# Two blocks in one kernel: the first convolution's weights and taps, and the even mixer's token stage

## The chip, the cores and the metric

One core of a Trainium2 chip runs the whole program. The metric is the device time of one execution in microseconds, as the median of several runs. A profiled execution gives the trace from which the views below are taken; its span runs from the first to the last instruction.

## The reference, cut to what matters

One sequence of 512 tokens with 1024 channels passes through two blocks of two layers each, in float32. The change touches the first layer of either block.

```python
def conformer_conv(x, ...):               # first block, first layer
    a, b = split(rmsnorm(x, g) @ pw1_w + pw1_b, 2)
    h = a * sigmoid(b)
    h = depthwise_causal_conv(h, dw_w) + dw_b      # 31 taps per channel
    h = silu(layernorm(h, ln_g, ln_b))
    return h @ pw2_w + pw2_b

def even_mixer(h, ...):                   # second block, first layer
    z = h @ w_in                          # u, v, q, k, vv and the forget logits
    u, v = gelu(z[..., :512]), gelu(z[..., 512:1024])
    log_f = log_sigmoid(f_logit + b_f)
    q, k = rms_norm(q, g_qn), rms_norm(k, g_kn)    # per head of 64
    y_a = u * (w_s . rms_norm(v) + b_s)   # inside blocks of 128 tokens
    y_b = softmax(q.k / 8 + c_t - c_s, causal) . vv, c = cumsum(log_f)   # 8 heads
    return concat(y_a, y_b) @ w_out
```

The first block ends with `rmsnorm(h, final_norm)`, and the second begins with `rms_norm(x, g_mix)`.

## The kernel before, in words

The stream x is held transposed: eight tiles of 128 channels by 512 tokens. Every product of full precision is done as three matmuls of fp32r halves, `mm3` (lines 242 to 245): high x high, high x low and low x high. `split` (lines 260 to 262) makes the two halves of a tile, the high one with ScalarE and the low one with VectorE. `wload` (from line 215) brings a weight tile with one transfer on SP's queue and splits it; the raw tiles have three buffers, the halves two.

The order of the instructions isn't the program's. The tile framework plans each engine's queue with a simulated timeline and takes, among what is ready, what stands first in the program. `behind(last)` (line 256) puts the instructions of its block behind `last` on that engine's queue. PSUM has eight banks of 128x512, which `banks` deals out to tags.

**Convolution** (lines 600 to 732). Eight chunks of x are loaded; `Norm.chunk` (from line 332) splits each, scaled by the gain, and sums the squares, partly on GpSimd, partly on ScalarE. The two weight tiles of block 0 are loaded on the same queue after chunks 1 and 4. `front(c)` does the two products of output block c (48 matmuls into two banks of tag "acc", which has three), multiplies both by R, the row of 1/rms per token, and gates them into `hp`. Block 0 comes without R: `rest()` loads the taps, forms the token sums with 128x1 matmuls (`token_sums`, line 279) and spreads the factors into R. `back(c)` does the 31 taps of block c. PE_TAPS of them run on TensorE, as three matmuls with a diagonal matrix that ScalarE makes from the identity (lines 655 and 656); then VectorE adds its taps into the same PSUM bank (tag "o", two banks; line 665), while GpSimd adds POOL_TAPS of products that ScalarE makes (lines 667 to 673). Line 677 joins both sums into `yc[c]` and so frees the bank. For the last block VectorE sums into `z`, so that it need not wait for TensorE, and line 675 joins it to GpSimd's `y`. Between the blocks TensorE also multiplies the memory's keys and values (tag "m", two banks), for later layers. Then follow the layer norm and the second product.

**Even mixer** (lines 1009 to 1205). `n4` is the norm between the blocks, with an outer factor: the first block's final norm has to be applied to x itself, and r0 is its 1/rms. `factors` forms both sums and r, r0; `row` spreads r into R and r0 into R0, and GpSimd multiplies the eight x by R0 (line 370). `token_linear` (line 1036) multiplies tokens by weights into four banks of tag "tok" (five); its weights come in four quarters of 24 matmuls. The first one is v. `head_norm` (from line 1054) takes such a product, scales it by r, sums squares by head on GpSimd and VectorE, and normalises. In order of the program: v, u, keys, queries, forget gates, the gating by `w_s`, values. `rsqrt` uses a power on GpSimd and four small VectorE operations (lines 273 to 277).

The attention's logits of a head (`weights`, line 736) are, for each of four query tiles, three matmuls into a bank of tag "s": two for q.k, from xh and xl, and one for the cumulated forget gate, with `selh` as the selecting matrix and `cs` as the values. `cs` has rows 0 to 7 and 32 to 39, in a tile of 64 partitions; the rest of it is zero. The query tiles have 128, 256, 384 and 512 columns. Then VectorE adds the mask and takes the minimum, ScalarE the exponential, GpSimd scales, TensorE transposes and applies the values (`apply`, line 759). The products with the first half of `w_out` have no need of the heads and fill TensorE between them.

Of the kernel before, what the change touches and what calls it, by code (L numbers as in the profile page):

```python
# [15 lines left out]
S = 512  # L16
D = 1024
DC = 8
# [4 lines left out]
PE_TAPS = (10,) * 5 + (12, 14, 18)  # L23
POOL_TAPS = (6,) * 8
# [109 lines left out]
def tile_kernel(ctx, tc, I, out):  # L134
# [9 lines left out]
    def nm(s):  # L144
        uid[0] += 1
        return f"{s}_{uid[0]}"
# [25 lines left out]
    def tmp(shape, tag, bufs=None, dt=FT, pool=None):  # L172
        return (pool or tp).tile(shape, dt, tag=tag, name=nm(tag), bufs=bufs)
# [105 lines left out]
    def token_sums(accs, n=S // 128, o=None):  # L279

        o = ps(n, tag="st") if o is None else o
        for j in range(n):
            for i, acc in enumerate(accs):
                T.matmul(o[:, j:j + 1], acc[:, j * 128:(j + 1) * 128], ones[:, 0:1], start=i == 0, stop=i == len(accs) - 1)
        return o
# [35 lines left out]
    class Norm:  # L321
# [17 lines left out]
        def factors(self, last=None):  # L339
# [18 lines left out]
            if self.outer:  # L358
                V.tensor_tensor(self.r, self.r, self.r0, op=OP.mult)

        def row(self, R=None, parts=False, last=None):

            with behind(last):
                R = tmp([128, S], "R", 1) if R is None else R
                A.activation(R, spread(self.r, parts=parts), AF.Copy)
                if self.outer:
                    R0 = tmp([128, S], "t", TB)
                    A.activation(R0, spread(self.r0), AF.Copy)
                    for c in range(DC):
                        G.tensor_tensor(x[c], x[c], R0, op=OP.mult)  # L370
            return R

# [228 lines left out]
    first = []  # L601
    for c in range(DC):
        nc.sync.dma_start(x[c], I["xt"][c])
        if c in (1, 4):
            first.append(wload(I["w_pw1"][0, len(first)], 8, 128))
        n0.chunk(c)
    n1 = Norm("ffn_norm", 0, quick=())
    with phase("conv") as p, banks(acc=3, st=1, o=2, m=2):
        yc = [p.tile([128, S], FT, name=f"yc{c}") for c in range(DC)]
        s1, s2, mark = [], [], {}  # L610
        with phase("conv_a") as q:
# [6 lines left out]
            def rest():  # L618
                nc.sync.dma_start(wd, I["taps"])
                split(wdh, wdl, wd)  # L620
                n0.finish(R)

            def front(c):

                o = []
                for j in range(2):
                    w = wload(I["w_pw1"][c, j], 8, 128) if c else first[j]
                    o.append(ps())
                    lin(o[j], w, xh, xl)
                if c == 0:  # L630
                    rest()
                sb = tmp([128, S], "t", TB)
# [376 lines left out]
    with phase("even") as p, banks(t=2):  # L1009

        selh = p.tile([64, 8, 128], FR, name="selh")
# [7 lines left out]
        cs = p.tile([64, S], FR, name="cs")  # L1019
# [5 lines left out]
        with banks(tok=5, st=1):  # L1025
            with phase("even_p") as q:
# [9 lines left out]
                def token_linear(src):  # L1036

                    o = [ps(tag="tok") for _ in range(4)]
                    for u in range(4):
                        wh, wl = wload(src[u], 2, 512)  # L1040
                        for k in range(2):
                            for j in range(4):
                                t = slice(128 * j, 128 * j + 128)
                                last = mm3(o[j], xh[:, 2 * u + k, t], xl[:, 2 * u + k, t], wh[:, k], wl[:, k], u + k == 0, u == 3 and k == 1)
                        token_linear.last.append(last)
                    return o

                token_linear.last = []
                first = token_linear(I["w_em"][0])
                n4.factors(token_linear.last[0])  # L1050
                R = n4.row(parts=True, last=token_linear.last[3])
# [60 lines left out]
                head_norm(token_linear(I["w_em"][1]), 8, AF.Copy, queries)  # L1112
                with phase("even_f") as q2:
# [299 lines left out]
```

## Time and profile before

| | before |
|---|---|
| runs, us | 2489.91, 2494.72, 2497.57 (median 2494.72) |
| profiled execution, us | 2492.68 |
| its span, us | 2490.8 |
| TensorE busy | 2435.1 us, 98% |
| weight loads busy | 2112.4 us, 85% |
| VectorE busy | 2027.5 us, 81% |
| ScalarE busy | 1272.5 us, 51% |
| GpSimd busy | 396.7 us, 16% |
| granted TensorE clock, mean | 0.993 |

The profiled execution's own time is 1.9 us more than its span. Busy shares are means over the whole kernel; the views below are taken from the stretches that change, in us from the span's start. PE is TensorE, PEld its weight loads, DVE VectorE, ACT ScalarE, POOL GpSimd, SP the engine that issues transfers. The matmuls overlap: a row's duration is longer than the step to the next one, so their pace is read from the starts.

### The profile page before, as it was taken

To read this page: it belongs to the slowest core of one execution; us is meant where nothing else is said; L and a number is where in the kernel's file an instruction comes from. 1 tells how busy PE (TensorE), PEld (TensorE's weight loads), DVE (VectorE), ACT (ScalarE), POOL (GpSimd) and SP (SyncE) were. 2 spreads that over 40 slices of the span, in tenths; PEclk is the share of its full clock that TensorE was granted. 3 is DMA by queue.
4 is the path that set the end of the run, shared out by engine and by line. 5 is a ranking of instruction groups with operands and counts; after the bars stand their busy time and mean duration, and the time that the engine had idled before them with its cause. 6 is when DMAs were issued, how large, how long until landed. Compare 5 with 4: busy or idle time off the path is not lost.

```text
span 2490.8 us, 37986 instructions
## 1 busy us (share of the span) xinstructions
PE 2435.1 (98%) x14133; PEld 2112.4 (85%) x14133; DVE 2027.5 (81%) x3511; ACT 1272.5 (51%) x2182; POOL 396.7 (16%) x444
## 2 busy tenths in 40 slices
PE   8998999999999999999999999999999999999999
PEld 6876899998777879999977778899999888799998
DVE  6896899886688869998765877799987766899885
ACT  6674544444577845444453566644444325644442
POOL 3781000000134400000014544000000014000000
PEclk9999999999999999999999999999999999999999
DMA  4122333332400033333322123333333222333332
GB/s 139 60 68 85 106 100 113 103 102 73 130 30 15 1 98 94 111 106 105 100 77 76 51 68 132 124 105 105 103 102 106 69 92 94 97 101 108 102 102 77
DMA packets 82712, 226.11 MB, mean 91 GB/s; under 512 B 9440, under 2 KB 20192, under 8 KB 82272
## 3 DMA queue, kind: packets, MB, share of 16 engines
q1 hardware_dynamic: 82528, 223.69, 28.6%
q8 instruction: 112, 1.84, 0.3%
q14 instruction: 72, 0.59, 0.1%
HBM read 216.31 MB, written 4.19 MB: 89 GB/s over the span
## 4 chain that ended last, share of the span: by engine, by line
PE 86%; DVE 7%; POOL 2%; issue 2%; ACT 1%; DMA 1%; SPq 0%; DVEq 0%; POOLq 0%; ACTq 0%
PE fi L244 12%; PE fi L245 12%; PE fi L243 12%; PE fo L243 6%; PE fo L244 6%; PE fo L245 6%; PE acc L245 6%; PE acc L243 6%; PE acc L244 6%; PE s L746 2%; DVE wl L262 2%; PE tok L244 1%; PE tok L245 1%; PE t L769 1%; PE tok L243 1%
## 5 line engine op out<-in xcount | busy, mean ns | idle before, releaser
L261 ACT ACTIVATE wh<-wr 128x1024 fp32r<-128x1024 f32 (+2 forms) x435 | 360.4, 833 | 595.8 <-PE fo L244 184.7
L262 DVE TENSOR_TENSOR wl<-wr,wh 128x1024 fp32r<-128x1024 f32 (+2 forms) x431 | 419.3, 975 | 95.6 <-ACT wh L261 91.5
L244 PE MATMUL fo<-hl,wh 128*128 128x512 f32 x704 | 275.2, 391 | 0.0
L245 PE MATMUL fo<-hh,wl 128*128 128x512 f32 x704 | 275.0, 391 | 0.0
L243 PE MATMUL fo<-hh,wh 128*128 128x512 f32 x704 | 272.8, 391 | 0.0
L243 PE MATMUL fi<-th,wsh 128*128 128x256 f32 x912 | 257.6, 282 | 0.0
L244 PE MATMUL fi<-tl,wsh 128*128 128x256 f32 x912 | 257.4, 282 | 0.0
L245 PE MATMUL fi<-th,wsl 128*128 128x256 f32 x912 | 257.2, 282 | 0.0
L245 PE MATMUL fi<-xh,wl 128*128 128x256 f32 (+1 forms) x800 | 246.9, 309 | 0.0
L244 PE MATMUL fi<-xl,wh 128*128 128x256 f32 (+1 forms) x800 | 246.7, 309 | 0.0
L262 DVE TENSOR_TENSOR wsl<-ws,wsh 128x1024 fp32r<-128x1024 f32 x152 | 185.6, 1221 | 74.9 <-ACT wsh L261 74.8
L243 PE MATMUL fi<-xh,wh 128*128 128x256 f32 (+1 forms) x800 | 245.9, 308 | 0.0
L261 ACT ACTIVATE wsh<-ws 128x1024 fp32r<-128x1024 f32 x152 | 161.1, 1060 | 73.8 <-PE fi L244 73.6
L243 PE MATMUL acc<-xh,wh 128*128 128x512 f32 x416 | 166.6, 403 | 11.6 <-ACT wh L261 9.3
L244 PEld LDWEIGHTS fi<-tl,wsh 128*128 128x128 f32 x912 | 174.1, 191 | 1.1
L245 PEld LDWEIGHTS fi<-th,wsl 128*128 128x128 f32 x912 | 174.2, 191 | 0.6
L243 PEld LDWEIGHTS fi<-th,wsh 128*128 128x128 f32 x912 | 174.1, 191 | 0.7
L501 DVE TENSOR_TENSOR x<-fo,x 128x512 f32<-128x512 f32 x192 | 131.1, 684 | 49.2 <-PE fo L245 48.4
L245 PE MATMUL acc<-xh,wl 128*128 128x512 f32 x416 | 167.5, 403 | 2.3 <-DVE wl L262 2.2
L244 PE MATMUL acc<-xl,wh 128*128 128x512 f32 x416 | 166.1, 400 | 0.0
L243 PEld LDWEIGHTS fi<-xh,wh 128*128 128x128 f32 x800 | 151.0, 189 | 12.1
L244 PEld LDWEIGHTS fi<-xl,wh 128*128 128x128 f32 x800 | 150.3, 188 | 12.2
(507 smaller groups left out, 6326.2 us busy)
## 6 DMA issues: line engine op xcount, KB each, us to landing
wr<-in_w_fin_dram SPq DMA_DIRECT2D x88, 512.0 KB, 3.5
wr<-in_w_sin_dram SPq DMA_DIRECT2D x88, 512.0 KB, 3.6
wr<-in_w_fout_dram SPq DMA_DIRECT2D x64, 256.0 KB, 2.7
wr<-in_w_sout_dram SPq DMA_DIRECT2D x64, 256.0 KB, 2.7
wr<-in_w_pw_dram SPq DMA_DIRECT2D x24, 512.0 KB, 3.7
wr<-in_w_xkv_dram SPq DMA_DIRECT2D x16, 512.0 KB, 3.6
wr<-in_w_em_dram SPq DMA_DIRECT2D x16, 512.0 KB, 3.5
wr<-in_w_fout_dram SPq DMA_DIRECT2D x32, 192.0 KB, 2.6
```

What stands on the lines that cost most here:

```text
L243: T.matmul(o, lh, rh, start=start, stop=False)
L244: T.matmul(o, lh, rl, start=False, stop=False)
L245: return T.matmul(o, ll, rh, start=False, stop=stop)
L261: A.activation(h, src, AF.Copy)
L262: V.tensor_tensor(l, src, f32(h), op=OP.subtract)
L501: V.tensor_tensor(x[m], o, x[m], op=OP.add)
L746: T.matmul(o, qs(i), keys[:, :n], start=a == 0, stop=a == len(pairs) - 1)
L769: T.transpose(ot[:, a:a + 128], tiles[i][:, 128 * j:128 * j + 128], ident)
```

## The change

In the convolution PE_TAPS goes from 94 to 104 taps in all (blocks 0 to 4 get two more each), POOL_TAPS from 48 to 46 (two fewer in the last block), and VectorE's share from 106 to 98. The two weight tiles of block 0 come in halves of four k, issued by ScalarE, ahead of the chunks in the program; their splits are of 512 columns. Block 0's two products are walked together over k. Block 1's products use the two banks "m" and stand behind block 0's token sums on TensorE.

In the even mixer the token sums of `n4` stand between the third and the last quarter of the first product, the Gelu table is loaded as soon as r is there, and `row` no longer multiplies x. That is done by `stream`, called after the queries: VectorE multiplies x by R0 in PSUM. `selh` and `cs` get 128 partitions, the new ones zero.

```diff
--- before.py
+++ after.py
@@ -20,8 +20,8 @@
 FC = 22
 EPS = 1e-6
 TAPS = 31
-PE_TAPS = (10,) * 5 + (12, 14, 18)
-POOL_TAPS = (6,) * 8
+PE_TAPS = (12,) * 6 + (14, 18)
+POOL_TAPS = (6,) * 7 + (4,)
 BIG = 1e30
 
 BLOCKS = (3, 3, 4, 4, 4, 4)
@@ -281,7 +281,8 @@
         o = ps(n, tag="st") if o is None else o
         for j in range(n):
             for i, acc in enumerate(accs):
-                T.matmul(o[:, j:j + 1], acc[:, j * 128:(j + 1) * 128], ones[:, 0:1], start=i == 0, stop=i == len(accs) - 1)
+                token_sums.last = T.matmul(o[:, j:j + 1], acc[:, j * 128:(j + 1) * 128], ones[:, 0:1], start=i == 0,
+                                           stop=i == len(accs) - 1)
         return o
 
     def spread(r, tag="st", parts=False):
@@ -357,18 +358,20 @@
             rsqrt(self.r, a, 4)
             if self.outer:
                 V.tensor_tensor(self.r, self.r, self.r0, op=OP.mult)
+            return token_sums.last
 
         def row(self, R=None, parts=False, last=None):
 
             with behind(last):
                 R = tmp([128, S], "R", 1) if R is None else R
                 A.activation(R, spread(self.r, parts=parts), AF.Copy)
-                if self.outer:
-                    R0 = tmp([128, S], "t", TB)
-                    A.activation(R0, spread(self.r0), AF.Copy)
-                    for c in range(DC):
-                        G.tensor_tensor(x[c], x[c], R0, op=OP.mult)
             return R
+
+        def stream(self):
+
+            R0 = spread(self.r0)
+            for c in range(DC):
+                V.tensor_tensor(x[c], x[c], R0, op=OP.mult)
 
         def finish(self, R=None, row=True, parts=False):
             self.factors()
@@ -598,11 +601,18 @@
 
 
     n0 = Norm("a_norm", 0, quick=(1, 3, 5))
-    first = []
+
+    first = [[wp.tile([128, 1024], dt, tag="w" + e, name=nm("w" + e), bufs=b) for e, dt, b in
+              (("r", FT, WR), ("h", FR, WH), ("l", FR, WH))] for _ in range(2)]
+    halves = slice(0, 512), slice(512, 1024)
+    for h, half in enumerate(halves):
+        for j, (raw, _, _) in enumerate(first):
+            nc.scalar.dma_start(raw[:, half].rearrange("p (k m) -> p k m", k=4), I["w_pw1"][0, j, :, 4 * h:4 * h + 4])
     for c in range(DC):
         nc.sync.dma_start(x[c], I["xt"][c])
-        if c in (1, 4):
-            first.append(wload(I["w_pw1"][0, len(first)], 8, 128))
+        if c in (0, 3):
+            for raw, hi, lo in first:
+                split(hi[:, halves[c // 3]], lo[:, halves[c // 3]], raw[:, halves[c // 3]])
         n0.chunk(c)
     n1 = Norm("ffn_norm", 0, quick=())
     with phase("conv") as p, banks(acc=3, st=1, o=2, m=2):
@@ -618,17 +628,25 @@
             def rest():
                 nc.sync.dma_start(wd, I["taps"])
                 split(wdh, wdl, wd)
-                n0.finish(R)
+                n0.factors()
+                rest.sums = token_sums.last
+                n0.row(R)
 
             def front(c):
 
-                o = []
-                for j in range(2):
-                    w = wload(I["w_pw1"][c, j], 8, 128) if c else first[j]
-                    o.append(ps())
-                    lin(o[j], w, xh, xl)
+
+                o = [ps(tag="m" if c == 1 else "acc") for _ in range(2)]
                 if c == 0:
+                    for k in range(DC):
+                        for j, (_, hi, lo) in enumerate(first):
+                            s_ = slice(128 * k, 128 * k + 128)
+                            mm3(o[j], hi[:, s_], lo[:, s_], xh[:, k], xl[:, k], k == 0, k == DC - 1)
                     rest()
+                else:
+                    for j in range(2):
+                        w = wload(I["w_pw1"][c, j], 8, 128)
+                        with behind(rest.sums if c == 1 and j == 0 else None):
+                            lin(o[j], w, xh, xl)
                 sb = tmp([128, S], "t", TB)
                 V.tensor_tensor(sb, o[1], R, op=OP.mult)
                 A.activation(sb, sb, AF.Sigmoid, bias=col("a_pw1_b", 8 + c))
@@ -1008,7 +1026,8 @@
 
     with phase("even") as p, banks(t=2):
 
-        selh = p.tile([64, 8, 128], FR, name="selh")
+        selh = p.tile([128, 8, 128], FR, name="selh")
+        G.memset(f32(selh[64:128]), 0.0)
         for a in (0, 32):
             A.activation(selh[a:a + 32], ident[a:a + 32, a:a + 8].unsqueeze(2).to_broadcast([32, 8, 128]), AF.Copy)
         mask = p.tile([128, S], FT, name="mask")
@@ -1016,7 +1035,7 @@
         G.affine_select(mask, mask, [[-1, S]], OP.is_ge, BIG, base=384, channel_multiplier=1)
         gqn = p.tile([128, 1], FT, name="gqn")
         V.tensor_scalar(gqn, col("e_g_qn_2"), -0.125, None, op0=OP.mult)
-        cs = p.tile([64, S], FR, name="cs")
+        cs = p.tile([128, S], FR, name="cs")
         G.memset(f32(cs), 0.0)
         yh = p.tile([128, 4, S], FR, name="yh")
         yl = p.tile([128, 4, S], FR, name="yl")
@@ -1033,22 +1052,24 @@
                 wsl = q.tile([128, 4, 128], FR, name="wsl")
                 split(wsh, wsl, wsr)
 
-                def token_linear(src):
+                def token_linear(src, between=None):
 
                     o = [ps(tag="tok") for _ in range(4)]
+                    last = None
                     for u in range(4):
                         wh, wl = wload(src[u], 2, 512)
-                        for k in range(2):
-                            for j in range(4):
-                                t = slice(128 * j, 128 * j + 128)
-                                last = mm3(o[j], xh[:, 2 * u + k, t], xl[:, 2 * u + k, t], wh[:, k], wl[:, k], u + k == 0, u == 3 and k == 1)
-                        token_linear.last.append(last)
+                        with behind(between(last) if between and u == 3 else None):
+                            for k in range(2):
+                                for j in range(4):
+                                    t = slice(128 * j, 128 * j + 128)
+                                    last = mm3(o[j], xh[:, 2 * u + k, t], xl[:, 2 * u + k, t], wh[:, k], wl[:, k],
+                                               u + k == 0, u == 3 and k == 1)
+                    token_linear.last = last
                     return o
 
-                token_linear.last = []
-                first = token_linear(I["w_em"][0])
-                n4.factors(token_linear.last[0])
-                R = n4.row(parts=True, last=token_linear.last[3])
+                first = token_linear(I["w_em"][0], n4.factors)
+                table(AF.Gelu_apprx_tanh, n4.r)
+                R = n4.row(parts=True, last=token_linear.last)
                 r = n4.r
 
                 def head_norm(o, groups, func, done):
@@ -1110,6 +1131,7 @@
 
                 head_norm(token_linear(I["w_em"][2]), 8, AF.Copy, keys)
                 head_norm(token_linear(I["w_em"][1]), 8, AF.Copy, queries)
+                n4.stream()
                 with phase("even_f") as q2:
                     fw = q2.tile([128, DC, 128], FR, name="fw")
                     fraw = q2.tile([128, DC, 8], FT, name="fraw")
```

## Rows read from the trace of the kernel before

**Rows 1.** Waits of TensorE, 0 to 225 us: total us, times, longest us.
```profile
PE acc L243 <- ACT wh L261: 8.5, 1, 8.5
PE o L243 <- DVE yc L677: 4.7, 1, 4.7
...
PE acc L243 <- DVE t L633: 1.9, 1, 1.9
```

**Rows 2.** Busy time by stretch, convolution: PE, PEld, DVE, ACT, POOL, clock, DMA.
```profile
40.00:160.00 120.00, 120.00 (x516) 96.56 (x516) 107.18 (x139) 85.19 (x192) 87.24 (x71) 1.00 0.22 67
160.00:180.00 20.00, 15.11 (x57) 11.60 (x56) 19.96 (x25) 15.97 (x45) 13.26 (x9) 0.83 0.14 51
```

**Rows 3.** Waits of TensorE, 1260 to 1500 us.
```profile
PE tok L244 <- DVE wl L262: 6.3, 2, 3.6
PE tok L243 <- ACT tt L1062: 3.0, 1, 3.0
```

**Rows 4.** Busy time by stretch, the two attentions (columns as in rows 2).
```profile
1410.00:1460.00 50.00, 50.00 (x244) 35.83 (x243) 34.34 (x101) 32.40 (x91) 14.87 (x30) 1.00 0.04 11
750.00:850.00 100.00, 96.79 (x582) 80.85 (x580) 85.38 (x278) 83.61 (x231) 46.96 (x86) 1.00 0.02 7
```

**Rows 5.** Timeline, convolution's last block: start, duration, engine, line, tiles, wait.
```profile
172.63 0.77 PE L243 MATMUL o<-ch,dgt 128*128 128x512 f32 x1 [4.68 <-DVE yc L677]
...
176.97 0.39 PE L244 MATMUL o<-cl,dgt 128*128 128x512 f32 x1
...
187.91 1.76 DVE L675 TENSOR_TENSOR y<-y,z 128x512 f32<-128x512 f32 x1 [3.89 <-POOL y L673]
...
189.77 0.69 DVE L677 TENSOR_TENSOR yc<-o,y 128x512 f32<-128x512 f32 x1
```

**Rows 6.** Timeline, start of the kernel.
```profile
2.17 0.43 SPq L224 DMA_DIRECT2D wr<-in_w_pw_dram  x1
...
16.82 1.41 DVE L266 SCALAR_TENSOR_TENSOR xl<-x,vec,xh 128x512 fp32r<-128x512 f32 x2
...
22.55 0.40 PE L245 MATMUL acc<-xh,wl 128*128 128x512 f32 x1
```

**Rows 7.** Groups by line, 40 to 190 us: busy us, mean ns, idle us.
```profile
L665 DVE SCALAR_TENSOR_TENSOR o<-hp,wd,o 128x512 f32<-128x512 f32 x99 | 72.2, 750 | 4.3 <-PE o L245 3.0
L673 POOL TENSOR_TENSOR y<-y,u 128x512 f32<-128x512 f32 x38 | 56.5, 1491 | 5.1 <-ACT u L672 3.9
```

**Rows 8.** Timeline, token sums and the factor r.
```profile
1284.36 1.84 PE L284 MATMUL st<-ones,acc 128*128 128x1 f32 x16
...
1291.44 0.16 DVE L359 TENSOR_TENSOR n_r<-n_r,n_r 128x4 f32<-128x4 f32 x1
```

**Rows 9.** Timeline, before and beside the multiplication of x.
```profile
1306.20 0.16 DVE L274 TENSOR_TENSOR rs_t<-rs_y 128x8 f32<-128x8 f32 x1
...
1310.89 12.02 POOL L370 TENSOR_TENSOR x<-x,t 128x512 f32<-128x512 f32 x8 [1.25 <-ACT t L368]
...
1311.07 1.25 DVE L274 TENSOR_TENSOR rs_t<-rs_y 128x8 f32<-128x8 f32 x1
```

**Rows 10.** Busy time by stretch, token stage (columns as in rows 2).
```profile
1330.00:1368.00 38.00, 38.00 (x173) 30.84 (x172) 15.65 (x25) 14.64 (x19) 11.54 (x8) 1.00 0.27 84
1368.00:1407.00 39.00, 35.37 (x179) 29.34 (x178) 37.23 (x51) 23.36 (x35) 25.96 (x16) 0.96 0.28 76
```

**Rows 11.** Tile selh (count, ns min/median/max, first to last), then the timeline beside it.
```profile
L746 PE MATMUL s<-cs,selh x32: 323/410/498, 1407.3 to 1458.0; 64*128 64x128 f32 x8, 64*128 64x256 f32 x8, 64*128 64x384 f32 x8, 64*128 64x512 f32 x8
...
1422.06 0.40 PE L746 MATMUL s<-xl,YS 128*128 128x512 f32 x1
1422.39 0.49 PE L746 MATMUL s<-cs,selh 64*128 64x512 f32 x1
1422.81 0.50 PE L775 MATMUL o<-th,V4f 128*128 128x512 f32 x1
1423.15 0.22 PE L746 MATMUL s<-xh,YS 128*128 128x128 f32 x1
```

## The prediction

> **What bounds the kernel now.** I read the waits of TensorE first, then busy time by stretch, then groups, then the timeline at each wait. In the convolution TensorE has three stops worth a name: 8.5 us before its first matmul, 1.9 us for VectorE's `t` (line 633) and 4.7 us for VectorE's `yc` (line 677) [rows 1]. Between 40 and 160 us it never stops: 516 matmuls in 120 us, 0.2326 us each, with VectorE busy for 107 us and GpSimd for 87 [rows 2]. In 160 to 180 us VectorE is full (19.96 of 20) and TensorE is not, and its granted clock is 0.83 [rows 2]. So this stage changes its bound: first TensorE's stream, then VectorE's taps. In the even mixer's token stage TensorE waits 6.3 us in two stops for the low half of a weight tile and 3.0 us for `tt` [rows 3]. In its attention no wait of note is listed, TensorE is busy 50 of 50 [rows 4], so the time there is the matmuls' own pace. A stop costs more than itself: after the 4.7 us, ten matmuls took 176.97 - 172.63 = 4.34 us instead of 2.33, at half the clock (1.2 instead of 2.4 GHz), 2.0 us more [rows 5]. After the shorter stops I take 1.5.
>
> **Convolution.** *First weights.* Today a block's split is one 1024-wide piece and block 0 runs to its end before block 1. With halves and both blocks walked together over k, TensorE can start on half a block, and its last six matmuls follow the last `xl`. That one ends at 18.23 us, so 18.23 + 6 x 0.2326 = 19.6 us is the floor for a phase that now ends at 22.95 [rows 6]: at best -3.3 us. The other end is 0, if the chunks are late anyway; nothing makes it a loss but two issues more, 0.43 us each [rows 6]. They go to ScalarE's queue, which has no transfers so far; they leave SP's, so that x's later chunks are issued two places sooner. I take -2.5, near the floor, since VectorE's chain and not the weights sets the end. The page "DMA: Bandwidth & Descriptors" of the Trainium skill (Issuing engines are not separate DMA queues) says that a second queue saves only issue time; no row here separates the two queues, and by it this term would be about 0 and the whole 2472.5.
> *Block 1 before R.* Front(1) now takes the two "m" banks, so it needs no bank that R frees: the stop of 1.9 and its slow start of 1.5 go, -3.4. If another wait took its place it would be the next bank, which R frees some 11 us (48 x 0.2326) later than the sums; R is there by then.
> *Ten taps to TensorE.* Three matmuls each, 30 x 0.2326 = +7.0 us, on an engine without a gap in 40 to 160 us: all on the path. ScalarE builds 20 more diagonals; it idles 34.8 of these 120 us [rows 2], and even at a VectorE tap's 0.75 us [rows 2, 7] they are 15, so I charge nothing; uncovered, that is up to 15.
> *VectorE's relief.* Blocks 0 to 4 lose two taps each there, 10 x 0.75 = 7.5 us [rows 7]. VectorE releases the bank for block 7's taps, and TensorE waited 4.7 for it; the two new changes ahead of it cancel the added taps for TensorE (-5.9 + 7.0), so it arrives 1.1 later and VectorE 7.5 earlier: stop and slow start go, -6.7. Ends: 0 and -6.7.
> *Tail.* Block 7 loses two GpSimd taps (2 x 1.49) and gains two VectorE ones (2 x 0.75) [rows 7]. VectorE idled 3.89 us there for GpSimd's `y`, so `yc` came at 190.46 [rows 5], while the last tap was out at about 176.97 + 44 x 0.2326 = 187.2. With `y` ready first, `yc` follows the last tap by its own 0.7 us and loses 2.2 to 2.6; I take -2.2, the other end is 0.
> Sum of the stage: -2.5 - 3.4 + 7.0 - 6.7 - 2.2 = -7.8.
>
> **Token stage.** *Sums earlier.* The token sums ran at 1284.36, after the whole first product; r was there at 1291.60 [rows 8]. They now stand before its last quarter, 24 matmuls or 5.6 us earlier, and the Gelu table is loaded once r is there instead of ahead of the first `tt`. The stop of 3.0 for `tt` goes, and 1.5 behind it: -4.5. What is queued behind the sums is that last quarter; it would wait if VectorE's sums were late. Ends 0 and -4.5; I take all of it, as 5.6 exceeds 3.0.
> *Stream factor.* GpSimd's eight multiplications took 12.02 us. Beside them a 128x8 VectorE operation took 1.25 instead of 0.16 us [rows 9], and the stop of 6.3 - 3.6 = 2.7 us for `wl` follows that jam. With them gone, -2.7 - 1.5 = -4.2. VectorE instead does 8 x 0.69 = 5.5 us (one of its 128x512 operations, the 0.69 of [rows 5]) and four scalings by the identity. In 1330 to 1368 us VectorE is busy for 15.65 of 38 us [rows 10], so I cost them at nothing: the planner has 22 us of room after r0 and before the first x is added. Without that cover they fall into 1368 to 1407, where VectorE is busy 37.23 of 39, and cost 5.5 + 1.5.
> *Third stop.* The 3.6 us [rows 3] lies in that full stretch. I leave it as it is: 0, between -5.1 (gone) and +7.0.
> Sum: -8.7. The memsets are GpSimd's, which is idle for 26 of the 38 us [rows 10]; uncovered they are one small operation each.
>
> **Attention.** A full 512-wide matmul steps 0.2326 us. The one before `selh` stepped 1422.39 - 1422.06 = 0.33, `selh` itself (64 rows) 0.42, the one behind it 0.34 [rows 11]: 0.10 + 0.19 + 0.10 = 0.39 too much, in each of 32 groups (all widths taken alike), 12.4 us. At 128 rows nothing sets these three apart from their neighbours. Upper end -12.4. The other end comes from the first block's attention, the same pipeline with no such matmul: there TensorE is busy 96.8 of 100 with VectorE and ScalarE at 85 and 84, while here they are at 69 and 65 [rows 4]. 34.34 / 0.854 = 40.2 us is what these 50 could shrink to before VectorE is as full as there, so -9.8 in 50 is near a cap; waits between heads of 1 us each would leave -4. I take -8, between the cap and that.
> The page "TensorEngine Tiling (Array Packing)" of the Trainium skill (Overview, Theoretical Speedup) speaks against this edit: a contraction of up to 64 rows can run up to twice as fast, so widening would give that up. Here the 64-row matmul took 0.42 where a full one steps 0.23, so the trace doesn't agree; the same page (Tiling Modes, Key Properties) says that a change of tiling mode drains the engine, and that the trace does show, on both sides of it.
>
> **Sum.** -7.8 - 8.7 - 8 = -24.5 us. The profiled execution took 2492.68; the median of the three runs is 2.0 above it. 2494.7 - 24.5 = 2470.
>
> **Rivals.** *Taps on the full engine* (0.13): the front is bound by x's chunks and the relief of VectorE ends in another wait (GpSimd is busy 87 of 120 us), so the stage gains nothing: 2478. For it: TensorE has no gap for 7 us. Against: VectorE is what it waited for. *Attention gives it back* (0.10): heads wait for VectorE and ScalarE as in the first block, or 64 rows are the cheaper form (half a step for 32 matmuls, some -2.5 us lost): gain 0 to 3, 2477 to 2480. *Stream in the full stretch* (0.08): +7.0, 2477. *Order elsewhere* (0.07): the planner orders the whole program anew; `behind` orders only TensorE's own queue, so the changed parts may not start when they say. Two of the gains fail or are paid back by some five new stops of 3 + 1.5: 2488 to 2494. *Slower* (0.04): with 20% of its work gone, TensorE runs dry in attention and each head becomes a chain that nothing fills, with the stop and the half clock of [rows 5], 6.7 us a head. Eight heads are +54 and the 8 lost, 2532; 2478 + 4 x 6.7 = 2505 is past the bound of 2502, so it is slower from four heads on. Against: the first block's attention keeps a granted clock of 1.00 [rows 4].
>
> **Numbers.** The forecast has 0.58, with a range of its own from 2462 to 2479 (attention between -12 and -4, the third stop, the start). The four rivals beside it end below 2481 in 0.31. A measurement of this kernel can tell 0.3%, 7.5 us, so faster means below 2487.2: 0.87, counting a little off for the tails; same 0.09, slower 0.04. The range 2461 to 2485 takes in the forecast and the first three rivals.
>
> **What would show it.** First matmul before 8.0 us; no stop near 31; no wait of `o` for `yc` line 677 above 1 us; the first matmul of the pointwise product after the convolution some 8 us before 210. In the even mixer no wait for `tt`, no GpSimd run of eight x, steps of 0.23 around `selh`, and attention some 8 us shorter. It is wrong if TensorE stops for `wl` longer than 6.3 us in the token stage, if a new wait stands at block 7, or if attention keeps its length with waits for `a_mn` or `p`.

## The result and the profile after

The changed kernel takes 2476.69 us (median of 4 runs, 2476.0 to 2477.16) against 2493.23 for the one before (4 runs): ratio 0.9932, interval 0.9915 to 0.995, so 16.5 us or 0.7% faster. The forecast was 24.5 us. The profiled execution has a span of 2474.6 us; before it was 2490.8, which leaves 16.1. Where they come from is read off the first matmul of each stage in the two timelines:

| first matmul of, us | before | after | gained so far |
|---|---|---|---|
| the first ffn (`fi`): end of the convolution | 263.73 | 264.44 | -0.7 |
| the token stage (`tok`) | 1248.15 | 1247.95 | 0.2 |
| the attention's first `selh` | 1407.29 | 1397.82 | 9.5 |
| the last values (`V4f`) of the attention | 1472.40 | 1457.07 | 15.3 |
| the next ffn | 1589.40 | 1573.73 | 15.7 |

So the convolution gave nothing, the token stage 9.3 and the attention 5.9 us; these are single profiles, and the section on the experiments says how far such times scatter. The waits of TensorE from 0 to 225 us after the change (total us, times, longest):

```profile
PE acc L243 <- ACT xh L265: 6.3, 1, 6.3
PE st L296 <- DVE t L295: 3.4, 2, 2.6
PE m L244 <- DVE wl L262: 2.7, 2, 2.4
PE st L284 <- DVE s L704: 2.6, 1, 2.6
PE m L243 <- ACT wh L261: 1.7, 1, 1.7
```

Against [rows 1] the stops for `yc` and for `t` in front of block 1 are gone, and the first matmul is 2.2 us earlier. But there are new stops: 1.7 us for `wh`, the split of block 1's weight, 2.6 for the sum `s` behind the last block, and 2.6 for `t` in front of the layer norm's second spread (line 296). The kernel before had one stop of 3.7 us at that norm, for another `t` (line 575). Busy time by stretch, the first row the first blocks, the others to be held against [rows 2, 4] (PE, PEld, DVE, ACT, POOL, clock, DMA share, GB/s):

```profile
6.00:42.00 36.00, 32.52 (x114) 23.55 (x115) 26.09 (x45) 28.89 (x61) 10.73 (x10) 0.91 0.47 164
160.00:180.00 20.00, 20.00 (x87) 16.15 (x86) 19.86 (x21) 16.46 (x48) 12.44 (x9) 1.00 0.11 35
1410.00:1460.00 50.00, 47.53 (x263) 38.80 (x262) 38.13 (x103) 36.14 (x94) 15.60 (x32) 0.97 0.13 43
```

From 160 to 180 us TensorE is now full, 87 matmuls in place of 57, at a clock of 1.00. In the attention it does 263 in 50 us in place of 244, with VectorE and ScalarE busier by some 4 us each. From 6 to 42 us it did 114 matmuls; the kernel before has this row:

```profile
6.00:42.00 36.00, 30.90 (x115) 22.99 (x116) 25.33 (x42) 25.29 (x53) 9.88 (x8) 0.95 0.49 178
```

With 115 there, the early start was spent before 42 us. The timeline of the changed kernel shows where (TensorE, then ScalarE):

```profile
21.28 0.40 PE L245 MATMUL acc<-xh,wl 128*128 128x512 f32 x1
21.51 0.95 PE L284 MATMUL st<-ones,acc 128*128 128x1 f32 x8
24.12 0.50 PE L243 MATMUL m<-xh,wh 128*128 128x512 f32 x1 [1.67 <-ACT wh L261]
24.46 0.39 PE L244 MATMUL m<-xl,wh 128*128 128x512 f32 x1
25.61 2.05 PE L296 MATMUL st<-t,ones 128*128 128x512 f32 x2 [0.76 <-DVE t L295]
26.67 1.42 PE L243 MATMUL m<-xh,wh 128*128 128x512 f32 x1
27.88 0.63 PE L244 MATMUL m<-xl,wh 128*128 128x512 f32 x1
28.31 0.63 PE L245 MATMUL m<-xh,wl 128*128 128x512 f32 x1
...
16.00 3.62 ACT L673 ACTIVATE dgt<-ident,wdh 128x128 fp32r<-128x128 f32 x12
19.52 3.61 ACT L674 ACTIVATE dgt<-ident,wdl 128x128 fp32r<-128x128 f32 x12
23.03 1.99 ACT L261 ACTIVATE wh<-wr 128x1024 fp32r<-128x1024 f32 x2
```

Block 0 ends at 21.28 instead of 22.55 [rows 6]. ScalarE, however, has 24 diagonals for block 0's twelve taps ahead of the split and gets to it only at 23.03. Then R's spread stands third in TensorE's queue and holds block 1 up; the matmuls behind it step 28.31 - 27.88 = 0.43 us instead of 0.23, at half the clock; from 6 to 42 us the granted clock is 0.91 on average.

By 180 us the changed kernel has started 706 matmuls and the one before 676: the difference is just the 30 added ones, so the two are level ahead of the last block.

At the other end of the convolution (VectorE, then GpSimd):

```profile
166.83 7.83 DVE L683 SCALAR_TENSOR_TENSOR z<-hp,wd,z 128x512 f32<-128x512 f32 x5
174.58 0.74 DVE L683 SCALAR_TENSOR_TENSOR o<-hp,wd,o 128x512 f32<-128x512 f32 x1
175.24 1.12 DVE L683 SCALAR_TENSOR_TENSOR z<-hp,wd,z 128x512 f32<-128x512 f32 x1
...
178.64 0.74 DVE L683 SCALAR_TENSOR_TENSOR z<-hp,wd,z 128x512 f32<-128x512 f32 x1
...
186.09 1.29 DVE L695 TENSOR_TENSOR yc<-o,y 128x512 f32<-128x512 f32 x2
...
172.48 5.04 POOL L691 TENSOR_TENSOR y<-y,u 128x512 f32<-128x512 f32 x3
186.86 1.26 POOL L704 TENSOR_TENSOR s<-s,yc 128x512 f32<-128x512 f32 x1 [9.35 <-DVE yc L695]
```

Block 7's own taps (`z`) stand ahead of block 6's (`o`) on VectorE. Both `yc` come at 186 to 187 us: block 7's earlier than the 189.77 of [rows 5], block 6's later than before (183.3), and it is block 6's for which GpSimd idles 9.35 us.

In the even mixer one wait of [rows 3] is left, the third stop, and `tt` is gone (waits of TensorE, 1260 to 1500 us); the tile `selh` and the steps around it answer to [rows 11]:

```profile
PE tok L244 <- DVE wl L262: 3.7, 1, 3.7
PE acc L243 <- ACT wh L261: 1.1, 1, 1.1
```

```profile
L764 PE MATMUL s<-cs,selh x32: 273/308/393, 1397.8 to 1439.8; 128*128 128x128 f32 x8, 128*128 128x256 f32 x8, 128*128 128x384 f32 x8, 128*128 128x512 f32 x8
...
1410.16 0.40 PE L764 MATMUL s<-xl,YS 128*128 128x512 f32 x1
1410.40 0.39 PE L764 MATMUL s<-cs,selh 128*128 128x512 f32 x1
1410.62 0.40 PE L793 MATMUL o<-th,V4f 128*128 128x512 f32 x1
1410.86 0.22 PE L764 MATMUL s<-xh,YS 128*128 128x128 f32 x1
```

Steps of 0.24, 0.22 and 0.24 us stand where 0.33, 0.42 and 0.34 stood.

### The profile page after: what moved, and what is told of

It is laid out like the page before. It is cut to its first block, busy times and chain, and to the rows that moved or that the text cites. A ratio compares the mean times of both kernels' runs of the same rounds, so it can differ in the third digit from the quotient of the medians.

```text
span 2474.6 us, 38058 instructions
## 1 busy us (share of the span) xinstructions
PE 2428.0 (98%) x14163; PEld 2114.0 (85%) x14163; DVE 2025.8 (82%) x3513; ACT 1276.2 (52%) x2202; POOL 375.9 (15%) x435
## 3 DMA queue, kind: packets, MB, share of 16 engines
q8 instruction: 112, 1.84, 0.3%
## 4 chain that ended last, share of the span: by engine, by line
PE 87%; DVE 6%; issue 2%; ACT 2%; POOL 2%; DMA 1%; SPq 0%; DVEq 0%; ACTq 0%; POOLq 0%
PE fi L244 12%; PE fi L245 12%; PE fi L243 12%; PE fo L243 7%; PE fo L244 7%; PE fo L245 7%; PE acc L245 6%; PE acc L243 6%; PE acc L244 6%; PE tok L244 2%; PE tok L245 2%; PE tok L243 2%; PE s L764 1%; PE t L787 1%; DVE wl L262 1%
## 5 line engine op out<-in xcount | busy, mean ns | idle before, releaser
L262 DVE TENSOR_TENSOR wl<-wr,wh 128x1024 fp32r<-128x1024 f32 (+2 forms) x433 | 425.5, 985 | 89.5 <-ACT wh L261 88.7
L243 PE MATMUL acc<-xh,wh 128*128 128x512 f32 x400 | 158.1, 400 | 7.0 <-ACT xh L265 6.3
L245 PE MATMUL acc<-xh,wl 128*128 128x512 f32 x400 | 159.7, 400 | 2.4 <-DVE wl L262 2.4
L244 PE MATMUL acc<-xl,wh 128*128 128x512 f32 x400 | 159.6, 399 | 0.8 <-DVE xl L266 0.8
```

Of the source, the lines that this page charges most:

```text
L243: T.matmul(o, lh, rh, start=start, stop=False)
L244: T.matmul(o, lh, rl, start=False, stop=False)
L245: return T.matmul(o, ll, rh, start=False, stop=stop)
L262: V.tensor_tensor(l, src, f32(h), op=OP.subtract)
```

## The experiments

Every kernel was timed in five rounds beside the kernel before, and ratios are to that. The times of the reordered versions lie within 6 us of each other and their intervals overlap, so what tells them apart is the stage in the trace. There the first ffn starts between 263.30 and 265.58 us in the five profiles with the changed kernel's convolution, and between 263.36 and 266.12 in the three with the one before.

**The two halves of the change.** The first has only the convolution's hunks of the diff above, the second only the even mixer's, the third only this:

```diff
-        selh = p.tile([64, 8, 128], FR, name="selh")
+        selh = p.tile([128, 8, 128], FR, name="selh")
+        G.memset(f32(selh[64:128]), 0.0)
...
-        cs = p.tile([64, S], FR, name="cs")
+        cs = p.tile([128, S], FR, name="cs")
```

> The kernel before with the convolution part of the change alone (first weights by halves, both blocks together, block 1 in the m banks, the new tap tables). Theory: in the changed kernel the first matmul of the first ffn starts 0.7 us later than before, so the convolution part as a whole gains nothing: the span stays within 2 us of before, ratio 0.9995 to 1.001, and the same two new stops show, one near 23 us for the split of block 1's weights and one near 187 us for the sum with the last yc. Rival: the parts are planned together and spoil each other; alone the convolution gains the 7.8 us that were forecast, ratio 0.997.

> The kernel before with the even mixer's part alone (sums before the last quarter, x scaled by VectorE after the queries, the selecting matrix and its values on 128 partitions). Theory: it carries the whole gain, 9 to 10 us in the token stage and 6 in the attention, so the span is 15 to 17 us below before, ratio 0.9933 to 0.994, the same as the whole change. Rival: the convolution is worth the forecast 7.8 us and gives them back further on, for instance in the first ffn; then this one gains about 9, ratio 0.9965.

> The kernel before with the selecting matrix and its values on 128 partitions, the new ones zero, and nothing else. Theory: the 64-row matmul costs itself and the drain on either side, 0.39 us in each of 32 groups; half of the 12.4 us comes out at the end because the heads then wait elsewhere. The stretch from the first of these matmuls to the last application of the values goes from 65.1 to about 59 us, the span is 6 us shorter, ratio 0.9975. Rival 1: the attention gained in the changed kernel because the token stage before it no longer leaves work for it; then the widening alone gives under 2 us. Rival 2: it gives the whole 12.4, and another part of the change takes 6 of it back.

Measured: convolution alone 2492.71 us against 2492.38, ratio 0.9999 (0.9991 to 1.0008), with stops of 1.7 us for `wh` and 2.4 for `s`; even mixer alone 2475.86, 0.9929 (0.9916 to 0.9942); widening alone 2485.19, 0.9968 (0.9957 to 0.998). The theory holds in the first two: the convolution's part as a whole is worth nothing, and the even mixer's is worth the whole gain, a little past its size. In the third, attention went from 65.1 us (first `selh` to last `V4f`) to 56.8, and to 56.7 in the second: the widening gives 8.3 us, more than the theory's 6 and less than 12.4. Over all twelve runs with the wide form it is 56.6 to 59.3, and 61.5 in the last one, against 65.1 and 66.1 in the two with the narrow form, so the 59.3 of the changed kernel's profile is at the long end; it has a stop of 1.1 us for a weight there, and 3.4 us at half the clock beside it, that these two have not. Summed over the 32 groups, the three steps of `selh` and its neighbours take 27.7 us before and 17.4 with the widening alone: 10.3 us less, of which 8.3 come out at the last `V4f`.

**The ten taps.**

```diff
-PE_TAPS = (12,) * 6 + (14, 18)
-POOL_TAPS = (6,) * 7 + (4,)
+PE_TAPS = (10,) * 5 + (12, 14, 18)
+POOL_TAPS = (6,) * 8
```

> The changed kernel with the tap tables of before (94 taps on TensorE, 106 on VectorE, 48 on GpSimd). Theory: the trade is even. The added taps cost TensorE 7.0 us between 40 and 165, and 7.2 us of stops and half clock between 160 and 180 are gone; undone, the stop of about 4.7 us for yc comes back and the span stays within 1.5 us of the changed kernel, ratio 0.9994 to 1.0006. Rival 1: the taps are a plain cost, since the relief would have come from the new front alone: 7 us shorter, 0.997. Rival 2: VectorE's relief is worth more than the taps: 3 us or more longer, 1.0012.

Measured: 2475.06 us, 0.9925 (0.9912 to 0.9938), and the first ffn starts at 264.34 against 264.44. The stop is back (waits of TensorE, 0 to 225 us):

```profile
PE o L243 <- DVE yc L695: 4.7, 1, 4.7
```

So 7.0 us of taps bought 7.0 us of stops and slow matmuls (the 30 more from 160 to 180 us, at 0.2326): the trade is even, and by the stage both rivals fall; the times alone are too close to say so. One thing more shows here. With two taps fewer in block 0, ScalarE has 20 diagonals ahead of the split of block 1's weight instead of 24; the stop for `wh` is 0.6 us instead of 1.7, R's spread stands at 32.39 us instead of 25.61, and from 6 to 42 us TensorE does 123 matmuls instead of 114. Later stops take this back: behind the last block there is again one of 3.2 us for the `t` that the kernel before waited for.

**ScalarE's diagonals.** The last four taps' diagonals of block 0 go behind the split of block 1's first weight:

```diff
-        A.activation(h, src, AF.Copy)
+        split.hi = A.activation(h, src, AF.Copy)
...
+                        front.hi = front.hi or split.hi
...
-                    A.activation(dg[:, t % 4, 0], ident, AF.Copy, scale=f32(wdh[:, c, t:t + 1]))
-                    A.activation(dg[:, t % 4, 1], ident, AF.Copy, scale=f32(wdl[:, c, t:t + 1]))
+                    with behind(front.hi if c == 0 and t >= 8 else None):
+                        A.activation(dg[:, t % 4, 0], ident, AF.Copy, scale=f32(wdh[:, c, t:t + 1]))
+                        A.activation(dg[:, t % 4, 1], ident, AF.Copy, scale=f32(wdl[:, c, t:t + 1]))
```

> The changed kernel with the last four taps' diagonals of block 0 put behind the split of block 1's first weight on ScalarE. Theory: TensorE's stop of 1.7 us at 22.5 is ScalarE's 24 diagonals, 7.2 us of them ahead of that split; with 16 ahead of it the split starts at about 21.5 instead of 23.0, the stop is under 0.5 us, and of the 5.7 us that TensorE loses from 20 to 30 us some 2 to 3 go. VectorE is full from 160 to 188 us, so at the end of the stage 0 to 2 us of it are left: ratio to the changed kernel 0.999 to 1. Rival 1: the stop is bound to the release of the weight tiles by block 0's own last matmuls; it stays above 1.2 us. Rival 2: the gain comes through to the end, 2 to 3 us.

Measured: 2473.28 us, 0.9925 (0.9912 to 0.9937). No stop for `wh` is listed any more, and from 6 to 42 us TensorE did 134 matmuls, at a clock of 1.00:

```profile
6.00:42.00 36.00, 34.18 (x134) 25.21 (x135) 27.72 (x42) 28.98 (x62) 11.84 (x11) 1.00 0.57 193
```

That is 20 more than in the changed kernel, 4.7 us, and the first ffn starts at 261.19, 3.3 us earlier. Rival 2 holds by the stage: the gain comes through, with a little more than its size. The theory was wrong about block 7: VectorE is full there, but its work comes earlier with TensorE's (block 6's `yc` starts at 181.93 us instead of 186.09). The edit moved more than the split, though. R's spread stands here behind 26 of block 1's matmuls, in the changed kernel behind two:

```profile
29.61 1.02 PE L296 MATMUL st<-t,ones 128*128 128x512 f32 x2
```

**The queue of the first weights.**

```diff
-            nc.scalar.dma_start(raw[:, half].rearrange("p (k m) -> p k m", k=4), I["w_pw1"][0, j, :, 4 * h:4 * h + 4])
+            nc.sync.dma_start(raw[:, half].rearrange("p (k m) -> p k m", k=4), I["w_pw1"][0, j, :, 4 * h:4 * h + 4])
```

> The changed kernel with the four half transfers of the first weights issued by SP ahead of the chunks, not by ScalarE. Theory: the gain of 2.2 us at the first matmul is the second queue's: four issues of 0.43 us now stand ahead of x's first chunk, the first matmul starts at 7.7 to 8.2 us instead of 6.3, block 0 ends 1 to 1.7 us later and so does the stage. Rival: the gain is that of the halves; the first matmul stays within 0.5 us of 6.3 and the time within 1 us.

Measured: 2473.78 us, 0.9921 (0.9908 to 0.9935). The rival misses; the theory has the start nearly right, at 8.59 us a little past its range, and the stage wrong. The first matmul is 2.3 us later than in the changed kernel, block 0 ends 0.9 later (22.16), and yet the first ffn starts 3.6 us earlier, at 260.83. The first 40 us of its waits, and 6 to 42 us:

```profile
PE acc L243 <- ACT xh L265: 8.6, 1, 8.6
PE m L243 <- ACT wh L261: 1.8, 2, 1.6
```

```profile
6.00:42.00 36.00, 31.58 (x125) 24.77 (x126) 25.54 (x38) 24.21 (x51) 9.45 (x8) 1.00 0.49 179
```

The stop for `wh` is the same, but here the planner put R's spread further back, so block 1 ran on, and the clock stayed at 1.00:

```profile
33.00 1.02 PE L296 MATMUL st<-t,ones 128*128 128x512 f32 x2
```

An early first matmul is not what this stage lacks. In all six profiles of the new front with the spread behind two of block 1's matmuls, TensorE does 114 to 119 from 6 to 42 us; in the five with it behind 26 or more, 123 to 134. So the early spread, with the half clock around it, seems to cost more than the stop for `wh`. No run moves the spread alone, so the two shares aren't measured apart.

**The last block.**

```diff
-POOL_TAPS = (6,) * 7 + (4,)
+POOL_TAPS = (6,) * 8
```

> The changed kernel with GpSimd's six taps in the last block instead of four, so VectorE has seven there instead of nine. Theory: VectorE is full from 160 to 188 us, its taps in block 7 take 1.1 to 1.6 us each beside GpSimd, and they stand ahead of and between block 6's taps; with two fewer the yc of block 6 comes some 2.5 us earlier than 186.8, GpSimd's wait of 9.35 us for it and TensorE's 2.6 us for the sum shrink, and the stage is 1.5 to 3 us shorter. Rival: GpSimd's y is then late by two more steps of about 1.3 us, the wait for y of before comes back, and the stage is the same or longer.

Measured: 2475.63 us, 0.993 (0.9918 to 0.9943). Block 6's `yc` came at 184.5 instead of 186.8 and the stop for `s` fell from 2.6 to 0.6, as the theory says, but the first ffn starts at 264.57, no earlier. TensorE's waits from 180 to 215 us show what is late next:

```profile
PE m L243 <- ACT wh L261: 2.2, 2, 2.0
PE m L244 <- DVE wl L262: 1.6, 2, 1.1
PE m L243 <- ACT t L578: 1.2, 1, 1.2
PE st L284 <- DVE s L704: 0.6, 1, 0.6
```

The weights of the memory's products (`wh` and `wl` of tag "m") are late next there, not GpSimd's `y`; that they are what holds the stage is read from these waits, and no run removes them.

**The token stage's two edits, each undone.** In the first, `row` copies R0 and GpSimd multiplies x as before; in the second the sums stand behind the whole product:

```diff
-                n4.stream()
...
-                first = token_linear(I["w_em"][0], n4.factors)
+                first = token_linear(I["w_em"][0])
+                n4.factors(token_linear.last)
```

> The changed kernel with x multiplied by R0 as before: ScalarE copies R0 and GpSimd does the eight multiplications behind the row. Theory: the jam comes back; VectorE's small operations beside GpSimd's take over 1 us instead of 0.16, a second stop for wl of about 2.7 us with its slow start returns, and the token stage is 3.5 to 5 us longer. Rival 1: the jam only hurt because the sums stood late; with the sums early GpSimd's twelve microseconds hide and the time is within 1 us. Rival 2: VectorE's eight multiplications cost more in the full stretch than GpSimd's; then it is shorter by 1 to 3 us.

> The changed kernel with the token sums behind the whole first product instead of its third quarter. Theory: r comes 5.6 us later, TensorE stops again for the first tt, about 3 us and 1.5 of slow start, and the token stage is 3.5 to 5 us longer. Rival: the stop for tt came from GpSimd's eight multiplications and from the order of the Gelu table, not from the sums; then the time is within 1 us.

Measured: 2482.22 us, 0.9955 (0.9941 to 0.9968), and 2481.59, 0.9952 (0.994 to 0.9965). From the first `tok` to the first `selh`: 159.14 us before, 157.11 with the early sums alone, 154.51 with VectorE's multiplication alone, 149.87 with both. Undoing one costs 7.2 and 4.6. Between profiles of the same code this stage differs by up to 1.5 us. The 159.14 is one of three profiles with neither edit (157.66 to 159.14), so the early sums alone gain 0.6 to 2.0. Both theories hold, the first with more than its size; without the early sums TensorE waits 3.1 us for `tt` again. The jam with GpSimd's multiplication (GpSimd, TensorE, then VectorE):

```profile
1305.41 12.38 POOL L372 TENSOR_TENSOR x<-x,t 128x512 f32<-128x512 f32 x8
...
1316.71 0.80 PE L244 MATMUL tok<-wl,xh 128*128 128x512 f32 x1 [4.14 <-DVE wl L262]
...
1307.25 1.25 DVE L275 TENSOR_TENSOR rs_t<-rs_t,e_ss 128x8 f32<-128x8 f32 x1
1311.05 3.41 DVE L1095 TENSOR_TENSOR tt<-tt,e_rn 128x512 f32<-128x512 f32 x2
1314.38 2.28 DVE L262 TENSOR_TENSOR wl<-wr,wh 128x1024 fp32r<-128x1024 f32 x1
```

and the same small operation and the eight multiplications in the changed kernel:

```profile
1304.92 0.16 DVE L275 TENSOR_TENSOR rs_t<-rs_t,e_ss 128x8 f32<-128x8 f32 x1
1306.13 0.68 DVE L374 TENSOR_TENSOR x<-x,st 128x512 f32<-128x512 f32 x1
1306.80 4.27 DVE L374 TENSOR_TENSOR x<-x,st 128x512 f32<-128x512 f32 x7
```

**The third stop.** Six operations of VectorE go behind the split of a quarter of the value weights (`lo[-2]` the third, `lo[-1]` the fourth); the second and third kernel have ScalarE's reordering as well:

```diff
+                        token_linear.lo.append(split.lo)
...
-                    split(yh[:, g], yl[:, g], t)
+                    us[g] = t
...
+                for g in range(4):
+                    with behind(token_linear.lo[-2]):
+                        split(yh[:, g], yl[:, g], us[g])
...
-                    (G if c else V).tensor_tensor(xl[own, h], KT[own, c], f32(xh[own, h]), op=OP.subtract)
+                    with behind(None if c else token_linear.lo[-2]):
+                        (G if c else V).tensor_tensor(xl[own, h], KT[own, c], f32(xh[own, h]), op=OP.subtract)
```

> The changed kernel with six of VectorE's operations (the low halves of the four gated tiles and of the first two heads' keys) put behind the split of the third quarter of the value weights. Theory: the stop of 3.7 us that is left in the token stage is this split in VectorE's full queue: its high half is ready at 1373.7 us, the low one starts at 1380.8, and five of those operations, 4.6 us, stand between. With them behind it the stop is under 0.5 us and the token stage 4 to 5.4 us shorter; ratio to the changed kernel 0.998. Rival: VectorE is full, so what is put off is late next: the attention starts with a stop for the keys or the query halves, and the gain is under 1 us.

> The changed kernel with both reorderings, ScalarE's diagonals of block 0 behind the split of block 1's weight and VectorE's six operations behind the split of the value weights. Theory: the two stages are a thousand microseconds apart and add up: 3.3 and 4 to 5.4 us, 7 to 9 below the changed kernel, some 2468 us, ratio to before 0.990. Rival: one takes the place of the other through the order of the whole program; then 2471 to 2473.

> As the kernel with both reorderings, but VectorE's six operations stand behind the split of the fourth quarter of the value weights instead of the third's. Theory: putting them behind the third split only moved the stop to the fourth, whose high half was ready at 1379.8 us and whose low half started at 1386.5; with the six behind the fourth it starts some 2 us earlier, the stop of 4.6 us falls to 1 to 2.5 and the token stage gains 2 to 4 us, with the convolution's 3.3 some 2469 to 2472 us. Rival: VectorE's queue is simply full there; the query halves and normalised queries that now stand ahead of that split keep it as late, or the attention starts with a stop for the keys, and the time is that of the former, 2473 to 2475.

Measured: 2479.13 us, 0.9935 (0.9922 to 0.9948); 2474.22, 0.9919 (0.9905 to 0.9932); 2473.31, 0.9924 (0.9911 to 0.9938). The first theory falls. The third quarter's split is early, and the fourth's is late (VectorE, then TensorE); what is late next stands nearer than its rival said:

```profile
1376.05 1.19 DVE L262 TENSOR_TENSOR wl<-wr,wh 128x1024 fp32r<-128x1024 f32 x1
...
1386.51 1.23 DVE L262 TENSOR_TENSOR wl<-wr,wh 128x1024 fp32r<-128x1024 f32 x1
...
1387.79 0.79 PE L244 MATMUL tok<-wl,xh 128*128 128x512 f32 x1 [4.64 <-DVE wl L262]
```

In the second kernel the convolution's gain is there (first ffn at 261.64) and the token stage's isn't, so the two theories' sum falls with the first. In the last one the rival holds: the product itself is 4.5 us shorter than in the second (first to last `tok` 143.1 against 147.6 us), and the attention starts with what was put off (waits of TensorE, 1230 to 1500 us):

```profile
PE acc L245 <- DVE wl L262: 1.8, 2, 1.2
PE s L767 <- DVE V4f L266: 1.5, 2, 1.0
```

From the first `tok` to the last `V4f` the two take 209.6 and 210.0 us. VectorE is nearly full there in all three (31.7 to 32.7 of the 35 us from 1360 to 1395), and order alone moved the stop. No version is shown faster than the changed kernel. ScalarE's reordering has its 3 us in two of three profiles (first ffn at 261.19 and 261.64); in the third the front was already 2.4 us late at block 1 and it is 264.15.

## Why the prediction was right, and where it failed

The direction, the range and the whole even mixer were right; the convolution's -7.8 was not, and it is the difference between 24.5 and 16.5. What came is the first rival's time, the stage that gains nothing (2478 us), but not by its mechanism: VectorE's relief did end the stop in front of block 7, and what was lost was lost in front of block 1 and behind the last block. That 2476.69 also lies in the forecast's own range (2462 to 2479) is in part luck, since that range was made for the attention, the third stop and the start, not for a convolution without gain.

*First weights* (-2.5): the first matmul came at 6.31 us, as "before 8.0" asked, but block 0 ended 1.3 us earlier, and none of it was left at 42 us. The Trainium skill's page "DMA: Bandwidth & Descriptors" (Issuing engines are not separate DMA queues) says that a second issuing engine saves only the issue time. The trace comes near that: the four issues on SP took 1.84 us, and with them there the first matmul was 2.3 later. The 0 that the prediction drew from this for the stage came true for another reason, the stops in front of block 1.

*Block 1 before R* (-3.4): the step that failed. The stop for `t` went, but the prediction looked for its successor only among the banks. It stood on two queues: on ScalarE behind the diagonals, which the taps' step had "charged nothing" on a mean of idle time over 120 us, and on TensorE behind R's spread. The two added taps are four diagonals, at 0.30 us each 1.2 us, at the one place where nothing covers them; with the old tables the stop is 1.1 us shorter and the spread stands further back. The reordering takes eight diagonals out of the way, the spread moves back with it, and 3.3 us come out, nearly the whole term. But the kernel with SP's queue keeps all 24 and a stop of 1.6 us, has only the spread further back, and gains as much, though it starts later. By this comparison the early spread with its half clock, from 25.0 to 31.8 us, is the dearer of the two; why the planner put it there is not shown.

*Ten taps and relief* (+7.0 and -6.7): right, as the kernel with the old tables shows, but for the diagonals charged at nothing, which belong to the term above.

*Tail* (-2.2): wrong. Block 7's `yc` was indeed 3 us earlier, but block 6's came 2.8 later, and 2.3 of these went when GpSimd had its two taps back: a tap into `z` beside GpSimd took 7.83 / 5 = 1.57 us where the row used for it says 0.75. Even mended it shows no gain in the stage.

*Token stage* (-8.7): 9.3 in the trace. The split into -4.5 and -4.2 was too simple: one edit alone gives 2.0 or 4.6 and both give 9.3. With early sums the stop for `tt` goes, but GpSimd's multiplications come earlier too and fall on an earlier weight: TensorE stops behind 196 of the matmuls into `tok` instead of 220, for 4.14 us instead of 2.67, and 6.8 us at half the clock follow instead of 3.4. The eight multiplications took 4.95 us on VectorE and cost nothing, as forecast, though they ran at 1306 us and not in the stretch that the forecast had looked at; the third stop stayed.

*Attention* (-8): 5.9 in the changed kernel's profile and 8.3 with the widening alone. The cap of 9.8 and the floor of 4 both held. The upper end of 12.4 took all widths alike; the steps themselves lost 10.3. (The attention rival's own sum has a slip: a gain of 3 would end at 2475, not at 2477.) The Trainium skill's page "TensorEngine Tiling (Array Packing)" (Overview, Theoretical Speedup) gives a contraction of at most 64 rows up to twice the speed. The trace doesn't agree for a lone one, with full matmuls on either side: the 64-row form was the dear one. That the longer steps beside it are a drain of the engine, as the prediction says, is a reading; the trace shows only the steps.

## What to carry to other kernels

Idle time averaged over a stage covers nothing at its first block: before charging an engine's added work at nothing, look at what stands right behind it in that engine's queue. A stop removed is only gained when the next late thing has been found; here it was a split behind diagonals and a spread, then the memory's weights. Where an engine is nearly full, reordering its work may only move the stop, as three orders did here.

## What was not expected of the hardware

A VectorE tap that adds into PSUM took 0.74 us while GpSimd was at work; the same tap into an SBUF tile took 1.57 and 1.12, and 0.74 again once GpSimd had finished at 177.5. The Trainium skill says so on its page "SBUF — State Buffer" (Who interferes with whom): a VectorE instruction with two inputs in SBUF contends with a GpSimd instruction that reads SBUF, and one with at most one such input, outside the two-port modes, doesn't. The trace agrees in both cases, and in the 1.25 for 0.16 us of the token stage. But in the same jam a TENSOR_SCALAR of 128x8 with a single input in SBUF (`rs_t`, line 276) took 1.22 us, and 0.17 in the changed kernel; whether it ran in one of those modes no run shows.

Widening a matmul from 64 rows to 128, half of them zeros, made 32 of them and their neighbours 8.3 us cheaper, 0.26 us a group.
